# Row normalisation: the first tile's load split over two DMA queues

## The chip, the cores and the metric

One core of a Trainium2 chip runs the kernel. The metric is the device time of one execution in microseconds (us), as the median of several executions. The profile's span, from the first to the last instruction, is about 1.8 us shorter than the time (80.2 us of span in an execution of 82.04 us); the difference lies outside what the profile shows.

A ratio below is the mean time of one kernel's runs over the mean of the kernel before's runs on the same chip in the same rounds. It is therefore not quite the ratio of the medians that are quoted beside it. Brackets give its 95% interval.

## The reference

```python
x = np.random.randn(1024, 4096).astype(np.float32)      # axis=-1, eps=1e-12
norm = np.sqrt(np.sum(x ** 2, axis=-1, keepdims=True) + eps)
return (x / norm).astype(np.float32)
```

Each row of 4096 numbers is divided by its Euclidean norm. 16.78 MB are read and as many are written.

## The kernel before

Two tiles cover the input. A tile has 128 partitions, and each partition holds R = 4 whole rows of D = 4096 floats, which are 64 KiB in one contiguous run in memory. Both tiles have buffers of their own. All loads and stores are issued by SyncE. The first load is moved ahead of the program's entry barrier, the point at which the engines wait for one another before the body begins (in the trace before, SyncE issues this load at 0.00 us and the next one, behind the barrier, at 0.79; ScalarE and VectorE begin at 0.79 and 0.86).

```python
for i in range(n_tiles):                                  # n_tiles = 2
    g = RowGroups(nc, io, stats, scratch, D, R, eps_t)
    load = nc.sync.dma_start(out=g.flat(), in_=x_t[i])    # 8.39 MB
    if i == 0:
        first_load_to_front(nc, load.ins)                 # ahead of SyncE's entry drain
    groups.append(g)

for i, g in enumerate(groups):
    g.square_dve(R - 1)        # VectorE: sum of squares of row 3
    g.square_act(0)            # ScalarE: row 0
    g.norm(0)                  # sqrt on ScalarE, reciprocal on VectorE
    g.scale(0)                 # VectorE, in place
    g.square_act(1); g.norm(1); g.norm(R - 1)
    g.scale(1); g.scale(R - 1)
    g.square_act(2); g.norm(2)
    if i < n_tiles - 1:
        g.scale_by_both(2)     # 7/8 on ScalarE, 1/8 on VectorE
    else:
        g.scale(2)
    store = nc.sync.dma_start(out=out_t[i], in_=g.flat())
# ... (the last wait is handed to GpSimd)
```

## Time and profile before

| what | value |
|---|---|
| time, median of 3, later of 6 runs | 81.90 us, 81.88 us |
| DMA packets' share of 16 engines' span | 97.4% |
| VectorE, ScalarE busy | 33%, 37% |
| one 64 KiB packet in the steady part | 2.42 us |
| tile 0 landed, store 0 issued | 22.1 us, 38.99 us |

Read this table from the transfers down. The data pass through 16 DMA engines in packets, one of 64 KiB for each partition of a tile (512 of them for the four transfers of 128 partitions).

In the profile's lines DVE is VectorE, ACT is ScalarE and POOL is GpSimd; SPq and ACTq are the sequencers of SyncE and ScalarE, which issue the transfers, and L240 is a line of the kernel. A line of the windows has the window, its length, the busy time and number of instructions of VectorE, ScalarE and GpSimd, the granted clock, the DMA share and the GB/s. The packet records, which lie under the windows, give each packet's start, duration, size and queue, but not its engine: an engine's packets are followed by the fact that each begins where another ended (within 0.01 us in the steady part).

### The profile page before, as it was taken

Reading aid. Unit: us, or ns where it says so; the run is one execution under the profiler, and the core shown is the slowest. Engines: PE = TensorE matmul, PEld = TensorE weight load, DVE = VectorE, ACT = ScalarE, POOL = GpSimd, SP = SyncE. Lnnn points to the kernel's source line nnn. Section 1 sums busy time; section 2 is a strip of 40 time slices with the busy share of each in tenths; the row PEclk is TensorE's granted clock in tenths of the full one; section 3 lists DMA queues with packets and bytes.
Section 4 is the critical chain, followed back from the end, with each engine's and each line's share of the span. In section 5 each row is a group of like instructions: output and inputs, shape, how many; then the busy total and the mean of one; then the engine's idle time right before and its main releaser. Section 6 shows DMA issues by size and latency. Waiting matters only on the chain.

```text
span 80.2 us, 93 instructions
## 1 busy us (share of the span) xinstructions
DVE 26.7 (33%) x21; ACT 29.7 (37%) x23; POOL 0.2 (0%) x4
## 2 busy tenths in 40 slices
DVE  0000000000099599960039995999200000000000
ACT  6000000000099999989439999950000000000000
POOL 0000000000000000000000000000000000000000
DMA  9099996699996699996699990999991999992990
GB/s 490 33 523 523 523 490 294 261 523 523 523 490 261 294 523 523 523 490 261 294 523 523 523 490 33 523 523 523 523 458 65 523 523 523 523 425 98 523 523 0
DMA packets 576, 33.55 MB, mean 418 GB/s; under 512 B 64, under 2 KB 64, under 8 KB 64
## 3 DMA queue, kind: packets, MB, share of 16 engines
q1 hardware_dynamic: 576, 33.55, 97.4%
HBM read 16.78 MB, written 16.78 MB: 418 GB/s over the span
## 4 chain that ended last, share of the span: by engine, by line
DMA 51%; ACT 10%; DVE 9%; issue 0%
DMA xt<-in_x_dram 51%; ACT sq_act L33 9%; DVE xt L64 9%; ACT rstd L53 1%; DVE rstd L59 0%
## 5 line engine op out<-in xcount | busy, mean ns | idle before, releaser
L33 ACT ACTIVATE sq_act<-xt 128x4096 f32<-128x4096 f32 x6 | 21.7, 3609 | 22.4 <-DMA xt<-in_x_dram 22.4
L42 DVE SCALAR_TENSOR_TENSOR sq_dve<-xt 128x4096 f32<-128x4096 f32 x2 | 8.9, 4426 | 26.4 <-DMA xt<-in_x_dram 26.4
L64 DVE TENSOR_SCALAR xt<-xt,rstd 128x4096 f32<-128x4096 f32 x7 | 16.5, 2353 | 0.2
L72 ACT ACTIVATE xt<-xt,rstd 128x3584 f32<-128x3584 f32 x1 | 3.3, 3283 | 0.2 <-DVE rstd L59 0.2
L53 ACT ACTIVATE rstd<-ssq,eps_t 128x1 f32<-128x1 f32 x8 | 2.1, 290 | 0.1
L59 DVE RECIPROCAL rstd<-rstd 128x1 f32<-128x1 f32 x8 | 1.3, 160 | 2.5 <-ACT rstd L53 2.5
L33 ACT ACT_TABLE_LOAD x1 | 1.3, 1283 | 0.8 <-PEq L258 0.8
L53 ACT ACT_TABLE_LOAD x1 | 1.3, 1283 | 0.0
L33 ACT ACTIVATION_READ_ACCUMULATOR sq_act<-xt 128x1 f32 x6 | 1.1, 187 | 0.0
L78 DVE TENSOR_SCALAR xt<-xt,rstd 128x512 f32<-128x512 f32 x1 | 0.5, 487 | 0.0
L211 DVE MEMSET eps_t<- 128x1 f32 x1 | 0.1, 59 | 0.9 <-PEq L258 0.9
L42 DVE DVE_READ_ACCUMULATOR sq_dve<-xt 128x1 f32 x2 | 0.2, 83 | 0.0
L258 POOL MEMSET const-uint8-127<- 128x1 uint8 x1 | 0.1, 103 | 0.0
L258 POOL MEMSET const-bfloat16-1.0<- 128x1 bf16 x1 | 0.1, 102 | 0.0
L258 POOL MEMSET const-float32-0.0<- 128x1 f32 x1 | 0.1, 99 | 0.2 <-issue 0.2
L258 POOL MEMSET const-float32-1.0<- 128x1 f32 x1 | 0.1, 99 | 0.0
## 6 DMA issues: line engine op xcount, KB each, us to landing
xt<-in_x_dram SPq DMA_DIRECT2D x2, 31.3
out_dram<-xt SPq DMA_DIRECT2D x2, 22.5
```

Of the source, the lines that this page charges most:

```text
L33: self.nc.scalar.activation(out=sq_a, in_=self.x[:, r], func=ACT_F.Square, accum_out=self.ssq[:, r : r + 1],)
L42: self.nc.vector.scalar_tensor_tensor(out=sq_v, in0=self.x[:, r], scalar=1.0, in1=self.x[:, r], op0=ALU.mult, op1=ALU.mult, accum_out=self ...
L53: self.nc.scalar.activation(out=self.rstd[:, r : r + n], in_=self.ssq[:, r : r + n], func=ACT_F.Sqrt, bias=self.eps_t,)
L59: self.nc.vector.reciprocal(out=self.rstd[:, r : r + n], in_=self.rstd[:, r : r + n])
L64: self.nc.vector.tensor_scalar_mul(out=self.x[:, r], in0=self.x[:, r], scalar1=self.rstd[:, r : r + 1])
L72: self.nc.scalar.activation(out=self.x[:, r, :cut], in_=self.x[:, r, :cut], func=ACT_F.Copy, scale=rstd,)
L78: self.nc.vector.tensor_scalar_mul(out=self.x[:, r, cut:], in0=self.x[:, r, cut:], scalar1=rstd)
L211: nc.vector.memset(eps_t, eps)
L258: nc = _bacc.Bacc("TRN2", target_bir_lowering=False, num_devices=1)
```

## The change

The intent is to bring the first tile in by two transfers at once: rows 0 and 1 on SyncE's queue, rows 2 and 3 on ScalarE's, both issued ahead of the entry barrier.

```diff
-def first_load_to_front(nc, load):
+def to_front(nc, load):
 # ...
-            if i.engine == mybir.EngineType.SP and isinstance(i, mybir.InstDrain)
+            if i.engine == load.engine and isinstance(i, mybir.InstDrain)
 # ...
-        load = nc.sync.dma_start(out=g.flat(), in_=x_t[i])
         if i == 0:
-            first_load_to_front(nc, load.ins)
+            half = R * D // 2
+            for queue, part in ((nc.sync, slice(half)), (nc.scalar, slice(half, None))):
+                load = queue.dma_start(out=g.flat()[:, part], in_=x_t[i][:, part])
+                to_front(nc, load.ins)
+        else:
+            nc.sync.dma_start(out=g.flat(), in_=x_t[i])
```

## The prediction

81.9 us as it was, plus 0.1 us that was the estimate (nine more packets per engine at about 10 ns, from the closing packets of the trace before, which took 9 ns each), are 82.0 us. Two things that the prediction takes for granted were not shown by the trace before, which has one queue. That an engine takes turns between two queues is shown by the changed kernel's records: on all 16 engines the 32 KiB packets of load 0 alternate between the queues, 1.21 us apart. That a steady packet has no room below 2.42 us rests on what was seen: no 64 KiB packet of either kernel's first trace took less than 2.415.

> **What bounds the kernel now.** I read the page first, then the queue view, the chain of waits, the windows and the timeline. The page says that no compute engine is near its limit and that the transfers are:
>
> ```profile
> DVE 26.7 (33%) x21; ACT 29.7 (37%) x23; POOL 0.2 (0%) x4
> ...
> DMA packets 576, 33.55 MB, mean 418 GB/s; under 512 B 64, under 2 KB 64, under 8 KB 64
> ...
> q1 hardware_dynamic: 576, 33.55, 97.4%
> ```
>
> VectorE works for a third of the 80.2 us span, ScalarE for 37%, but the packets of the one queue fill 97.4% of the time of the 16 DMA engines. Of the 576 packets 64 are under 512 B: four transfers, 16 engines, one small closing packet each. The other 512 carry 33.55 MB, so 65,536 B each; an engine carries 32 of them, eight in each of the four transfers (load 0, load 1, store 0, store 1). So the kernel is 32 large packets in a row on each engine, plus a start and an end.
>
> The windows, in steps of 0.25 us, show the pace. The last two columns are the DMA share and the GB/s; a packet is booked whole in the window in which it begins (that is why a share passes 1), so GB/s times 0.25 us over 65,536 B counts the packets begun: 2884 is eleven, 1311 five, 262 one.
>
> ```profile
> 0.75:1.00 0.25, 0.06 (x1) 0.21 (x1) 0.00 (x0) 1.00 0.00 0
> 1.00:1.25 0.25, 0.00 (x0) 0.25 (x1) 0.00 (x0) 1.00 8.86 2884
> 1.25:1.50 0.25, 0.00 (x0) 0.25 (x1) 0.00 (x0) 1.00 1.47 524
> 1.50:1.75 0.25, 0.00 (x0) 0.25 (x1) 0.00 (x0) 1.00 0.64 262
> 1.75:2.00 0.25, 0.00 (x0) 0.25 (x1) 0.00 (x0) 1.00 0.71 262
> 2.00:2.25 0.25, 0.00 (x0) 0.07 (x1) 0.00 (x0) 1.00 0.60 262
> ...
> 4.00:4.25 0.25, 0.00 (x0) 0.00 (x0) 0.00 (x0) 1.00 3.02 1311
> ...
> 4.75:5.00 0.25, 0.00 (x0) 0.00 (x0) 0.00 (x0) 1.00 0.60 262
> ...
> 41.00:41.25 0.25, 0.00 (x0) 0.00 (x0) 0.00 (x0) 1.00 0.61 262
> ...
> 77.25:77.50 0.25, 0.00 (x0) 0.00 (x0) 0.00 (x0) 1.00 0.60 262
> ```
>
> A steady packet takes 3.02 x 0.25 x 16 / 5 = 2.42 us. The first of each engine is longer: 8.86 x 0.25 x 16 / 11 = 3.2 us for the eleven that begin first; the other five begin up to 1 us later. The last engine begins its second packet at about 4.80 (the packet records), its 17th at about 41.05 and its 32nd at 77.27. From 4.80 to 41.05 are 15 steps of 2.42 us: **this engine never pauses once it has begun**, and its last packet ends at 79.7, half a microsecond before the span does. So only two things move the end: when the slowest engine gets under way, and whether store 0 is there when that engine has finished load 1.
>
> The timeline and the queue's waits show how near the second thing is:
>
> ```profile
> 22.08 3.62 ACT L33 ACTIVATE sq_act<-xt 128x4096 f32<-128x4096 f32 x1 [20.01 <-DMA xt<-in_x_dram]
> 22.09 4.42 DVE L42 SCALAR_TENSOR_TENSOR sq_dve<-xt 128x4096 f32<-128x4096 f32 x1 [21.16 <-DMA xt<-in_x_dram]
> ...
> 35.68 3.28 ACT L72 ACTIVATE xt<-xt,rstd 128x3584 f32<-128x3584 f32 x1 [0.23 <-DVE rstd L59]
> ...
> 38.99 0.35 SPq L240 DMA_DIRECT2D out_dram<-xt  x1
> ```
>
> Load 0 lands at 22.1, both engines begin, and store 0 is issued at 38.99. By the packet records its packets begin on engines that were already free at 40.49 to 40.68, 1.5 to 1.7 us after the issue; those five engines lost about 0.2 us each, but the slowest is busy with load 1 until 41.05. Slack in tile 0's arithmetic: 41.05 less 40.68, some **0.4 us**, no more. The chain of waits ends in tile 1's arithmetic at 56.7, but store 1 is queued there behind store 0's packets until 60, so that part is not binding.
>
> [...]
>
> **The change, part by part.** Instruction order: SyncE's first issue shrinks to half the columns, ScalarE gains one issue ahead of everything, nothing else moves. Tile 0's waits split: the square of row 0 waits for the SyncE half, that of row 3, on VectorE, for the ScalarE half.
> - *Bytes*: the same. The 128 packets of load 0 become 256 of 32 KiB, and 16 closing packets are added. Each closing packet takes about 10 ns on its engine; if a large packet also carries an overhead of that order, eight more per engine plus a closing one are 0.1 us on the path.
> - *Issue*: ScalarE's takes some 0.35 us, from about 0.13 (where its entry drain stood) or after SyncE's at 0.38. The barrier falls some 0.1 to 0.4 us later and with it load 1's issue, now at 0.79; that waits behind 20 us of queue. Cost 0.
> - *Start of the engines*: the first descriptors still come from SyncE's issue at 0.00 and the first packets at about 1.0. I see no reason for the slowest engine to be much earlier: 0, with a small chance up to the spread of second starts, 4.80 less 4.02, 0.8 us.
> - *Landing of tile 0*: taking turns, both halves end within one small packet of each other (1.2 us), the SyncE half first; ScalarE may begin at about 21, VectorE at about 22.1 as before. ScalarE's early start reaches no store: on SyncE's queue store 0 stands behind load 1 anyway.
>
> Sum: +0.1 us of packets, 0 for the rest. 81.9 + 0.1 = **82.0 us**.
>
> **The rivals.**
> *A, the start is evened out.* Two queues feed an engine whose first packet was late from one of them. For it: five engines begin up to 1 us late and first packets take 3.2 us instead of 2.42.[...] If the slowest engine began its steady run with the fastest, 0.8 us would be gained: 81.1. Even a whole start without delay (second packet at 1.0 + 2.4 = 3.4 on every engine) would give 1.4 us, 1.7%; so faster by over 2% is nearly excluded.
> *B, load 1 pushes into tile 0.* Load 1 now stands behind only half of tile 0 on SyncE's queue. If ScalarE's half lags by more than one packet, SyncE's ring reaches load 1 first and a 64 KiB packet of 2.42 us slips in before the last 32 KiB packet. VectorE's square then begins at 24.5 and ends at 28.9; three scales at 2.35 plus 0.1 to 0.2 each end at 36.5; the last reciprocal and the 3.28 us share of ScalarE end at about 40.1, so store 0 is issued 1.1 us later. Less the slack of 0.4 that is 0.7 us: 82.6. With two such packets another 2.4: about 85. For it: SyncE is first in line[...]. Against it: the first 32 KiB takes at least 1.2 us, longer with the slow first packet, and the lag of issue is at most 0.4 us.
> *C, the first tile arrives in halves one after the other*, so that arithmetic begins near 12. The ScalarE queue would have to be starved; and tile 0's store would still wait behind load 1 on the SyncE queue. Time unchanged, 81.9.
>
> **Range and chances.** No effect within 0.3 us has about two thirds; A with 0.3 to 0.8 us gained about 12%; B with 0.4 to 1 us lost about 15%; B with two packets or something unforeseen over 1.6 us lost 6%. That gives 81.3 to 82.8 for eight in ten, 3% for faster by over 2% (below 80.3), 6% for slower (above 83.5), the rest within.
>
> **What would show it.** Right: a second queue with 128 packets of 32 KiB and about 12% of the engines' time, load 0 landing at 21 to 22.3, store 0 issued at 38.5 to 39.3, the last engine's packets without a gap. A right: first load 1 packets earlier and the span shorter by the same amount. B right: VectorE's first wait ends after 23, store 0's issue after 39.5, and windows near 41 without packets. Wrong altogether: 32 KiB packets much over 1.25 us in the middle of load 0, or a start of the first packet far from 1.0.

## The result

The changed kernel takes 82.00 us (81.77 to 82.09, 6 runs) against 81.88 us (81.73 to 81.99, 6 runs) before. The ratio is 1.0013 [0.9998, 1.0029]: the same.

The first fence is from the page of the changed kernel: packet counts, then packets, MB and share of the engines by queue.

```profile
DMA packets 720, 33.55 MB, mean 418 GB/s; under 512 B 80, under 2 KB 80, under 8 KB 80
q1 hardware_dynamic: 576, 29.36, 85.5%
q10 hardware_dynamic: 144, 4.19, 12.1%
```

A second queue has appeared with 128 large and 16 closing packets. Its 4.19 MB are missing from the first queue, and the two shares add up to 97.6%, where one queue had 97.4% before. The engines were full and are full.

The second is from the changed kernel's timeline (start, duration, engine, line, instruction, and in brackets how long the engine had waited and for what; a line marked x2 runs from the first of two merged instructions to the end of the second).

```profile
0.00 0.38 SPq L222 DMA_DIRECT2D xt<-in_x_dram  x1
0.13 0.36 ACTq L222 DMA_DIRECT2D xt<-in_x_dram  x1
...
21.96 3.62 ACT L33 ACTIVATE sq_act<-xt 128x4096 f32<-128x4096 f32 x1 [19.76 <-DMA xt<-in_x_dram]
22.14 4.43 DVE L42 SCALAR_TENSOR_TENSOR sq_dve<-xt 128x4096 f32<-128x4096 f32 x1 [21.09 <-DMA xt<-in_x_dram]
...
38.87 18.15 SPq L244 DMA_DIRECT2D out_dram<-xt  x2
```

The two issues overlap in time, and neither, at 0.38 and 0.36 us, is longer than the first issue was before (0.38). The halves land within 0.2 us of each other (the squares that wait for them begin at 21.96 and 22.14), at the time at which the whole tile landed before (22.08 and 22.09). Store 0 is issued 0.12 us earlier than before.

The third is from the windows of the changed kernel around the turn from load 1 to store 0, in the columns that the prediction explains.

```profile
40.25:40.50 0.25, 0.00 (x0) 0.00 (x0) 0.00 (x0) 1.00 1.24 524
40.50:40.75 0.25, 0.00 (x0) 0.00 (x0) 0.00 (x0) 1.00 5.53 2359
40.75:41.00 0.25, 0.00 (x0) 0.00 (x0) 0.00 (x0) 1.00 3.07 1311
41.00:41.25 0.25, 0.00 (x0) 0.00 (x0) 0.00 (x0) 1.00 0.00 0
```

All 16 engines have begun store 0 by 41.00, where one engine of the kernel before began it after 41.00. By the packet records the slowest engine begins at 40.90 instead of 41.05. In these two traces the load side is therefore 0.16 us quicker. That does not reach the end of the span, which is 80.2 us in both. The experiments ask first whether that small gain is real and was given back, and then what makes the splitting harmless.

### The profile page after: what moved, and what is told of

Same layout as the page of the kernel before. It is cut to its first block, busy times and chain, and to the rows that moved or that the text cites. A ratio compares the mean times of both kernels' runs of the same rounds, so it can differ in the third digit from the quotient of the medians.

```text
span 80.2 us, 97 instructions
## 1 busy us (share of the span) xinstructions
DVE 26.7 (33%) x21; ACT 29.7 (37%) x23; POOL 0.2 (0%) x4
## 3 DMA queue, kind: packets, MB, share of 16 engines
q10 hardware_dynamic: 144, 4.19, 12.1%
## 4 chain that ended last, share of the span: by engine, by line
DMA 50%; ACT 10%; DVE 9%; issue 0%
DMA xt<-in_x_dram 50%; ACT sq_act L33 9%; DVE xt L64 9%; ACT rstd L53 1%; DVE rstd L59 0%
```

## The experiments

Theory T is the prediction's: the end is the begin of the slowest DMA engine plus 32 packets of 2.42 us, and the split moves neither. Its first rival, G, is that the split starts the slowest engine 0.16 us earlier and that store 0 arrives too late to use it.

### Both kernels again

No edit, five rounds.

> The kernel before, unedited, timed against itself and traced again: what the chip's own scatter is. Theory T (the end is the slowest DMA engine's begin plus 32 packets of 2.42 us, and the split moves neither): ratio 1.000 within 0.002, and the last engine's second packet begins between 4.6 and 4.9 us, so the 4.80 (before) against 4.64 (after) of the first two traces is scatter or nearly so. Rival G (the split does start the slowest engine 0.16 us earlier and store 0 gives it back): the last second packet begins at 4.80 within 0.03 again, and so always later than in the changed kernel.

> The changed kernel, unedited, traced and timed again. Theory T: ratio 1.000 within 0.002; last engine past its first 64 KiB at 4.6 to 4.8. Rival G: at 4.64 within 0.03 again, load 1 done on the last engine at 40.9 again, and ten or more engines waiting for store 0's descriptors, with the span unchanged.

The kernel before against itself gave 81.84 us and a ratio of 1.0009 [0.9992, 1.0026]. The changed kernel gave 82.02 us, 1.0025 [1.0013, 1.0037]. By the packet records, the last engine to get past its first 64 KiB did so at 4.58 us before and 4.50 us after. So this moment moves by 0.22 us between two traces of the kernel before (4.80 and 4.58), and the difference between the kernels is 0.16 us in the first pair of traces and 0.08 in the second. Rival G's exact repetitions, at 4.80 and 4.64, did not come; theory T's bands, 4.6 to 4.9 and 4.6 to 4.8, were missed as well, by 0.02 and 0.10. T's ratio of 1.000 within 0.002 held for the kernel before and was just missed by the changed kernel, whose interval excludes 1. Rival G is not dead either: in both pairs the changed kernel was earlier at this point. What it loses again is the time from the last load packet's end to the last store packet's end, 38.78 and 38.79 us after, 38.64 twice before. In the changed kernel's two traces 13 and 4 engines had to wait for store 0's first packet (its record is then 2.45 to 2.47 us long, not 2.42), in the kernel before's 5 and 0. The later traces say more on both halves of G (see the part on the prediction below), but nothing here shows this to be the cause of the 0.1 to 0.25 us by which the changed kernel's medians lie above the kernel before's.

### Store 0 in two halves

```diff
+        if i == 0:                      # after g.scale(1)
+            nc.sync.dma_start(out=out_t[i][:, : 2 * D], in_=g.flat()[:, : 2 * D])
 # ...
-        store = nc.sync.dma_start(out=out_t[i], in_=g.flat())
+        if i == 0:
+            nc.sync.dma_start(out=out_t[i][:, 2 * D :], in_=g.flat()[:, 2 * D :])
+        else:
+            store = nc.sync.dma_start(out=out_t[i], in_=g.flat())
```

> The changed kernel with store 0 in two halves: rows 0 and 1 are stored as soon as they are scaled, issued near 32.4 instead of 38.9, so no engine can be idle between load 1 and store 0. Theory T: the slowest engine was hardly idle there, so at most 0.1 us is gained (ratio 0.999 to 1.001 against the kernel before). Rival G: the gain at the start, 0.16 us, is now kept, and the slower packets after an idle engine go too: 0.2 to 0.4 us gained (ratio 0.995 to 0.998).

It took 83.05 us, 1.0155 [1.0141, 1.0169], with the first half issued at 34.68 us. Both theories were wrong by more than a microsecond, in the same direction: here a store that was ready early went with a longer time.

### Both halves on one queue

```diff
-            for queue, part in ((nc.sync, slice(half)), (nc.scalar, slice(half, None))):
+            for queue, part in ((nc.sync, slice(half)), (nc.sync, slice(half, None))):
```

> Both halves of load 0 on SyncE's queue, ahead of the barrier: the packets of the changed kernel without the second queue. The halves now come one after the other, so the first lands near 12 us and ScalarE's first square begins near 12 instead of 22; VectorE, which begins with row 3, still begins at 22.1. Theory T: the total is unchanged (ratio 1.000 within 0.003), since tile 0's arithmetic is not what sets the end. A rival for which an early start of the arithmetic is worth something (the intent of splitting a load): 0.3 us or more gained. If packet size rather than the second queue sets the engines' start: the last engine past 64 KiB at 4.6 to 4.7, as in the changed kernel.

It took 83.15 us, 1.0169 [1.0155, 1.0184]: theory T and the rival, which had a gain, were both wrong. The timeline of this run shows that the arithmetic did start early, and that store 0 was issued seven microseconds sooner:

```profile
12.10 3.62 ACT L33 ACTIVATE sq_act<-xt 128x4096 f32<-128x4096 f32 x1 [9.56 <-DMA xt<-in_x_dram]
...
31.80 26.22 SPq L244 DMA_DIRECT2D out_dram<-xt  x2
```

The loss sits in one place. The window from 37.50 to 38.50 us is the one in which all 16 engines begin load 1's last packet (1049 GB/s times 1 us is 16 packets of 64 KiB). With 16 packets on 16 engines in a window of 1 us, the DMA share in the last column but one is at the same time the mean duration of these packets in microseconds. First this window of the changed kernel, then of the one-queue kernel:

```profile
37.50:38.50 1.00, 0.00 (x0) 1.00 (x1) 0.00 (x0) 1.00 2.42 1049
```

```profile
37.50:38.50 1.00, 0.00 (x0) 0.00 (x0) 0.00 (x0) 1.00 3.66 1049
```

The last packet of load 1 took 3.66 us instead of 2.42, on every engine (3.36 to 3.93 by the records), while the packet before it took 2.42 to 2.45. That is 1.24 us of the 1.38 lost. So a theory S was formed: when store 0 already lies in the queue behind load 1, it stretches load 1's last packet.

### Holding store 0 back

If S is right, useless work must make the one-queue kernel faster. Row 2's square was repeated on ScalarE in tile 0, with the result overwritten by the real one, so that store 0 is issued later.

```diff
+        if i == 0:
+            for cols in (4096, 4096, 1792):       # 512 or 1280 in place of 1792
+                g.square_act(2, cols)             # cols: how many columns are squared
         g.square_act(2)
```

> The one-queue kernel, 1.3 us slower than the kernel before with its store 0 issued at 31.8, given useless repeats of row 2's square on ScalarE (4096, 4096 and 1792 columns) so that store 0 is issued near 38.9, as in the kernel before. Theory S (store 0's descriptors, when they already lie behind load 1's last packet as that packet begins, stretch it from 2.42 to 3.4 to 3.9 us on every engine): the last packet of load 1 is back at 2.42 to 2.43 us and the time at 81.7 to 82.1 us, although more work was added. Rival O (the two issues in a row on one queue, ahead of the barrier, cost the time): still 83.0 to 83.3. Rival W (any early finish of tile 0's arithmetic is harmless, and the stretch comes of the packet sizes): still 83.0 or more.

> The same with 4096, 4096 and 512 columns repeated: store 0 issued near 37.7, so its descriptors reach the engines near 39.2, in the middle of load 1's last packet (38 to 40.4). Theory S as first put (what counts is whether they are there when that packet begins): no stretch, 81.6 to 81.9. If they need only be there some way before the packet ends: a part of the stretch, 82.0 to 83.0.

> The one-queue kernel with 4096, 4096 and 1280 columns repeated: store 0 issued near 38.2, between the 37.55 that stretched the last packets of load 1 by 0.5 to 0.9 us and the 38.67 that left them alone. Theory S with the cost falling steadily as the issue nears the packet's end: stretches of 0.1 to 0.5 us, 81.9 to 82.2. If there is a window without stretch and without idle engines: 81.6 to 81.75, a little faster than the kernel before.

The window of load 1's last packets, with 1792, 1280 and 512 columns in turn:

```profile
37.50:38.50 1.00, 0.00 (x0) 1.00 (x1) 0.00 (x0) 1.00 2.42 1049
```

```profile
37.50:38.50 1.00, 0.00 (x0) 0.66 (x1) 0.00 (x0) 1.00 2.48 1049
```

```profile
37.50:38.50 1.00, 0.00 (x0) 0.03 (x1) 0.00 (x0) 1.00 3.11 1049
```

| one-queue kernel, columns | store 0 issued, us | mean last packet of load 1, us | time, us | ratio |
|---|---|---|---|---|
| none | 31.80 | 3.66 | 83.15 | 1.0169 |
| 4096, 4096, 512 | 37.55 | 3.11 | 82.51 | 1.0085 |
| 4096, 4096, 1280 | 38.18 | 2.48 | 81.91 | 1.0010 |
| 4096, 4096, 1792 | 38.67 | 2.42 | 81.81 | 1.0012 |

Theory S holds, and its first wording does not. The store need not be there when the packet begins: issued at 37.55 and underway for 0.84 us at the least (the shortest of four later runs with idle engines; the 39.2 of the expectation was an estimate, 37.7 plus the 1.5 us that the prediction had read from the kernel before), it came after all those packets had begun (37.85 to 38.19), and the stretch is still 0.7 us. The cost falls as the issue comes nearer to the end of the packet, and from about 38.2 on it is lost in the scatter. Nine microseconds of added ScalarE work took 1.3 us off the time, so that tile 0's arithmetic is not what limits this kernel. The rivals O (two issues in a row) and W (packet sizes) are refuted, because those things were left as they were. The hoped-for window that beats the kernel before did not show: 81.91 us has a ratio of 1.0010 [0.9997, 1.0022].

### The split store on the kernel before

The same two-halves edit of store 0 was put on the kernel before.

> The kernel before (one transfer for load 0) with store 0 in halves, the first issued near 34.7. Theory S (a store queued behind load 1's last packet early stretches that packet): ratio 1.013 to 1.017, like the changed kernel with the same edit, because the first load's form has no part in it. If the stretch needed the second queue or the 32 KiB loads: ratio 1.000 within 0.002.

It took 82.97 us, 1.0138 [1.0124, 1.0151], with the same window reading as follows:

```profile
37.50:38.50 1.00, 0.00 (x0) 1.00 (x1) 0.00 (x0) 1.00 3.48 1049
```

The stretch belongs to the turn from loads to stores: in the first trace of the kernel before, load 1 was queued early behind load 0 (issued at 0.79 us) and store 1 behind store 0 (56.8), and the last large packets of load 0 took 2.42 us, those of store 0 2.42 to 2.45. With 3.48 us in this run, it needs neither the second queue nor the 32 KiB loads.

### Store 0 too late

```diff
+        if i == 0:
+            g.square_act(2, 1024)      # on the kernel before
         g.square_act(2)
```

> The kernel before with 1024 columns of row 2's square repeated in tile 0, so that store 0 is issued near 40.1 instead of 38.9, too late by my prediction's slack. The prediction's reading (a store's packets begin 1.5 to 1.7 us after its issue, slack 0.4 us): 0.6 to 0.8 us slower, 82.4 to 82.7. The later reading from the late-half run (on idle engines they begin 0.84 to 0.99 us after the issue; it is the load packet in progress that holds them back): the slack is 1 us, and the time is 81.8 to 82.1.

Store 0 was issued at 39.94 us. The time was 82.10 us, 1.0035 [1.0023, 1.0048], which is 0.26 us more than the 81.84 of its rounds. The windows of this run show all engines beginning store 0 together, after a pause:

```profile
40.50:40.75 0.25, 0.00 (x0) 0.00 (x0) 0.00 (x0) 1.00 0.02 0
40.75:41.00 0.25, 0.00 (x0) 0.00 (x0) 0.00 (x0) 1.00 9.21 3932
```

3932 GB/s times 0.25 us are 15 packets; by the records the first begins 0.84 us after the issue and the last 1.08 us. My slack of 0.4 us was too small, and the later reading's 1 us too large: 0.95 us of delay cost 0.26, which leaves about 0.7 us. With the earlier table this gives the whole picture of the turn: issued at 31.8 us, store 0 costs 1.3 us; from 38.2 to 39.0 nothing that can be told from the scatter; at 39.9 it costs 0.26. After that each microsecond costs one: in this run and in the three that follow store 0 is issued at 39.94, 42.92, 51.63 and 59.05 us, and the time is 42.1 to 42.2 us more in all four.

### What makes ScalarE's half harmless

Three runs put ScalarE's transfer at a disadvantage, from the crude to the fine. In the first, all of load 0 is on ScalarE's queue, so that load 1 on SyncE's no longer stands behind it.

```diff
-            half = R * D // 2
-            for queue, part in ((nc.sync, slice(half)), (nc.scalar, slice(half, None))):
-                load = queue.dma_start(out=g.flat()[:, part], in_=x_t[i][:, part])
-                to_front(nc, load.ins)
+            load = nc.scalar.dma_start(out=g.flat(), in_=x_t[i])
+            to_front(nc, load.ins)
```

> All of load 0 as one transfer on ScalarE's queue ahead of the barrier, load 1 on SyncE's after it. Theory T: load 0's and load 1's packets take turns from the second on, load 0 lands near 38 to 40 instead of 22.1, tile 0's arithmetic runs 17 us after that, the queues are empty from 41 until store 0 at 57, and the time is 96 to 100 us. Rival F (first come, first served on the engines): 81.8 to 82.2, since load 0 was issued 0.8 us earlier than load 1.

It took 101.26 us, 1.2383 [1.2361, 1.2405]. The timeline has tile 0's first square waiting for its data until load 1 is nearly in as well:

```profile
38.85 4.43 DVE L42 SCALAR_TENSOR_TENSOR sq_dve<-xt 128x4096 f32<-128x4096 f32 x1 [37.80 <-DMA xt<-in_x_dram]
...
59.05 10.96 SPq L242 DMA_DIRECT2D out_dram<-xt  x2
```

In this run the engines took turns between the queues, one packet each, from the third packet on (the records show 16 packets of one queue, then 16 of the other). The whole transfers were not served one after the other in the order of their issue: load 0, issued 0.79 us ahead of load 1, took 38.7 us to land, where it had landed at 22.1 in the kernel before. The time is 1.3 us beyond the expected range because tile 0's arithmetic took 20 us, not 17: here VectorE did tile 1's first square in the midst of it.

In the second run ScalarE's half is delayed by VectorE memsets that it has to follow (3.47 us for the long one).

```diff
+                if queue is nc.scalar:
+                    nc.vector.memset(sq_dve, 0.0)
+                    nc.vector.memset(g.x[:, 2, :1], 0.0)
+                    nc.vector.memset(g.x[:, 3, :1], 0.0)
                 load = queue.dma_start(out=g.flat()[:, part], in_=x_t[i][:, part])
-                to_front(nc, load.ins)
+                if queue is nc.sync:
+                    to_front(nc, load.ins)
```

> The changed kernel, but ScalarE's half of load 0 is issued late, behind a VectorE memset of a whole scratch row (2 to 4 us), after the barrier. Theory T (engines take turns between the queues, packet by packet; the changed kernel is safe because ScalarE's half lags by under one small packet): the ScalarE half ends behind two or three 64 KiB packets of load 1, lands 5 to 8 us later than 22.1, VectorE's first square begins at 27 to 30, store 0 is issued at 42.5 to 45.5, the engines stand idle for 3 to 6 us after load 1, and the time is 85 to 88 us. Rival F (the engines finish what came first, so a late half only lands a little late): 81.8 to 82.5.

It took 93.71 us, 1.1457 [1.1442, 1.1473]. Theory T had the mechanism right and the size wrong. The half was issued at 5.26 us, its first packets began at 8.75, and VectorE's square of row 3 at 36.40:

```profile
36.40 4.42 DVE L42 SCALAR_TENSOR_TENSOR sq_dve<-xt 128x4096 f32<-128x4096 f32 x1 [31.17 <-DMA xt<-in_x_dram]
```

By the records five packets of load 1 slipped in on 13 engines and six on three, where I had expected two or three. By an estimate from the 0.84 us that a store took to reach idle engines, most engines began two more packets of the other queue after this transfer could have arrived (6.1 us, 5.26 plus 0.84); what kept it waiting was not shown.

In the third run only the move ahead of the barrier is undone, for ScalarE's half alone.

```diff
-                to_front(nc, load.ins)
+                if queue is nc.sync:
+                    to_front(nc, load.ins)
```

> The changed kernel with only SyncE's half ahead of the entry barrier; ScalarE's half is its first instruction after the barrier, issued near 0.8 instead of 0.13. In the late-half run a half issued at 5.26 had its first packet at 8.75[...]. Theory T with that (call it T2): here ScalarE's first packet comes after SyncE's second or third, so one or two 64 KiB packets of load 1 slip into tile 0; VectorE begins at 24.5 or 27, store 0 is issued at 40 to 42.5, and the time is 82.2 to 84.5 us. If 0.7 us later in the issue is within the first packet's 1.9 us[...]: 81.8 to 82.1, like the changed kernel.

It took 85.09 us, 1.0394 [1.0378, 1.041], 0.6 us above T2's range. The timeline:

```profile
0.80 0.37 ACTq L222 DMA_DIRECT2D xt<-in_x_dram  x1
...
26.58 4.43 DVE L42 SCALAR_TENSOR_TENSOR sq_dve<-xt 128x4096 f32<-128x4096 f32 x1 [25.65 <-DMA xt<-in_x_dram]
...
42.92 0.35 SPq L245 DMA_DIRECT2D out_dram<-xt  x1
```

Issued 0.67 us later than in the changed kernel, ScalarE's half gets its first packet after SyncE's third instead of after its first (by the records at 5.11 us instead of 2.70). At the end of the tile one packet of load 1 then goes ahead of ScalarE's last large packet, and a second one ahead of the closing packet, the transfer's last (in the kernel before, load 0's last closing packet ends at 21.72 us and the first square begins at 22.08). VectorE begins 4.4 us later, and store 0 is issued 4.05 us later, when the engines have been empty for over two microseconds. The delay passes through ScalarE: its square roots wait 6.73 us for VectorE's square, and its squares of rows 1 and 2 stand behind them. This one edit, 0.67 us of issue, is all that separates the changed kernel, level with the kernel before, from one that is 3.9% slower.

No run beat the kernel before. What bounds it, 32 packets of 64 KiB (or the same bytes in 32 KiB ones) on every engine at 2.42 us each, is the same in all of them.

## Why the prediction was right or wrong

The forecast was no effect, at 82.0 us, and 82.00 us was measured. The mechanism, full DMA engines that the split doesn't unload (97.4% and 97.6% of their time), was right. The agreement to the hundredth is luck: the 0.1 us of the sum stood for packet overhead that came to 0.02, and what makes up the measured 0.12 is open. The steps fared as follows.

- **The bound** was right. The slowest engine's packets set the end in both kernels, and no experiment got under that.
- **Bytes**: right in count, 128 packets of 32 KiB, 16 closing packets and 12.1% of the engines' time. The 0.1 us was an overestimate: two steps of 1.2095 us (records of the middle of load 0) take 3 ns more than one of 2.416, so eight pairs cost some 0.02 us.
- **Issue**: right. ScalarE's took 0.36 us at 0.13, and load 1's moved from 0.79 to 0.92 us at no cost. The alternative, that it waits out SyncE's issue (to 0.38), did not happen.
- **Start of the engines**: about right; 0.08 and 0.16 us earlier in two pairs of traces, against a forecast of 0 with a chance of up to 0.8. The other traces show that this gain is no accident and that rival A had its reason wrong. With 32 KiB packets first, the last engine is past its first 64 KiB at 4.35 to 4.63 us in nine traces (mean 4.45), and four of these have one queue (4.35 to 4.49). With 64 KiB packets and load 0 on SyncE's queue it is at 4.57 to 4.80 in four traces (mean 4.64). The gain goes with the smaller packets and needs no second queue. It did not reach the end.
- **Landing of tile 0**: VectorE's begin at 22.1 was right. That ScalarE could begin at about 21, some 1.1 us earlier, was wrong: it gained 0.12 us. The records show why. SyncE's closing packet took a turn of its own, and ScalarE's last large packet went ahead of it: on the last engine SyncE's last large packet began at 19.15 us, ScalarE's at 20.36 and SyncE's closing packet at 21.57, and the square that waits for SyncE's half followed at 21.96.
- **"ScalarE's early start reaches no store"** failed as a general statement, and with it rival C's "time unchanged". The one-queue run made C true, with arithmetic from 12.10 us on, and it cost 1.3 us. I had seen that store 0 would stand behind load 1 and had taken standing there to be free. That the changed kernel was spared, because its arithmetic did not come early, is luck as far as this step goes.
- **Slack of 0.4 us**: too small. Store 0 reaches idle engines 0.84 to 1.08 us after its issue. The 1.5 to 1.7 us that I had read from the kernel before were measured on engines that were still at a load packet when the store was issued. An issue 0.95 us later cost 0.26 us, where the step gave 0.55.
- **Rival B** did not occur but exists. Two slipped packets were put at about 85 us, and the run with two took 85.09, partly by luck. The working let ScalarE go ahead and led the delay through VectorE's three scales, to a store 3.5 us later; in the run ScalarE's squares waited too, and the store came 3.9 us later than in the kernel before. The slack that was too small made up for that. Its counter-argument, that the lag of issue is at most 0.4 us, is what saved the change: at 0.13 us ScalarE's half takes the second turn, and at 0.80 it takes the fourth.

What stays open is why an early store stretches the load packet in front of it, and the exact source of the 0.1 to 0.25 us by which the changed kernel's median is above the kernel before's. A hint lies in the records: from the begin of store 0 on the last engine to the end of the last packet of store 1 pass 38.64 us in the four traces in which no engine waited for store 0 (the kernel before again and three one-queue runs), and 38.77 to 38.81 in the seven in which at least four did, two of them with one queue. The first trace of the kernel before, with five waiting engines and 38.64, doesn't fit, so this is not shown.

## What to carry to other kernels

Here the DMA engines were full from end to end (97.4% of their time before, 97.6% after), and splitting a transfer over two queues changed who went next and not how much went through: 81.88 and 82.00 us. The half that shared the engines with a later transfer on another queue was delayed as soon as it came two turns late (issued 0.67 us later, 85.09 us), so the order in a single queue was worth having. Work that finishes early is not always free: look at what it queues and behind what. Here a store issued at 31.80 us instead of 38.99 cost 1.3 us at the turn from loads to stores, and the timing of the kernel before happened to avoid that.
